# Small pads in SBUF that put the tiles of the three-product matmuls at multiples of 128 bytes

## The chip, the cores and the metric
One NeuronCore of one Trainium2 chip runs the whole program. The metric is the device time of one execution in microseconds. A difference under 0.5% is not told from none here.

## What is computed
A decoder trunk of two layers on 256 tokens of width 1024, in fp32. Cut to what matters:

```
for i in range(2):
    proj = x @ w_in[i]                      # q, k, v, u_ssm, u_pool, three gates
    h = sum(sigmoid(gate_b) * (branch_b @ w_br_b) for b in (attn, ssm, pool)) @ w_o[i]
    x = layer_norm(alpha * x + h)
    x = layer_norm(alpha * x + cross_attention(x, mem))   # 4 heads, 256 memory tokens
    f = swiglu(x)          if i == 0        # width 2816
    f = moe_swiglu(x)      if i == 1        # 8 experts of width 3584, the best 2 of each token
    x = layer_norm(alpha * x + f)
```

The 8 experts hold most of the weights: 336 of the 462 transfers of 1 MB.

## The kernel before
All weights are fp32 and come from HBM in tiles `raw` of 128 partitions x 2048 columns (1 MB), issued on SyncE's queue in the order of use. Up to the second layer's mixer `raw` is one of three buffers of the pool `fifo`; in that layer's cross-attention and in the experts eleven buffers `fx` and the tile `k1` come in turn with them (`wnew`, lines 244 to 257).

A product of fp32 accuracy is made of three fp32r products. Each half of `raw` (128 x 1024) is split once it is needed: ScalarE writes `whi`, the value rounded to fp32r (`hi_of`, line 218), and VectorE writes `wlo = raw - whi` (`lo_of`, line 221). Both have three buffers in the pool `wsp`. The activations are split in the same way (`xhi`/`xlo`, `m_hi`/`m_lo`, `u_hi`/`u_lo`, `hh`/`hl`, `xg0`/`xg1` and so on). TensorE then accumulates three products in PSUM:

```
def mm3(ps, whi, wlo, xhi, xlo, first, last):            # lines 281 to 283
    T.matmul(ps, whi, xhi, start=first, stop=False)
    T.matmul(ps, whi, xlo, start=False, stop=False)
    return T.matmul(ps, wlo, xhi, start=False, stop=last)
```

`T.matmul(out, a, b)` loads `a` (128 columns) as the stationary operand and moves the columns of `b` past it; the trace names them `out<-b,a`. Two arrangements occur. In `mm3` (projections, gates, branches, the gate and up parts of the dense SwiGLU) the weights are stationary and 256 columns of activations move. In `xs_step` (lines 428 to 432) and `mm3_x` (lines 450 to 452) the activations are stationary and 512 (once 256) columns of weights move; `gate_up` of the experts (lines 1301 to 1303) does the same and its `down` calls `mm3_x`. `prepare` gathers an expert's tokens by 128 matmuls with a matrix of ones and zeros (line 1273, 256 columns) and `scatter` puts them back by 64 of 512 columns (lines 1338 and 1339). A few plain fp32 matmuls (attention scores in line 1067, weighted values in line 1100, transposes, the state space) are not split.

Line 238 is the helper `Line`, which keeps a sequence in order; many operations have it as their line. Around the three-product matmuls, attention and the state space are woven into the gates' and branches' projections (`weave`, line 956). The order of each engine's instructions is set when the program is built and is the same for every run.

SBUF is handed out by pools. A pool's tiles lie behind each other along a partition, each rounded up to 32 bytes, and the next pool begins where the last one ends; pools with `side="right"` (`wa`, `kv`, `gg`) grow downwards from the upper end. So a few small tiles in one pool (`halfpi` and `mhalf` in `cp`, the statistics of `sm`, the parameters in `sc`, the routing values of `moe`) set where all pools behind it begin. Slices of the tiles that the fp32r matmuls read begin at multiples of 512 bytes from the tile's start, so a tile's start modulo 128 is that of all its operands.

Of the kernel before, what the change touches and what calls it, by code (L numbers as in the profile page):

```python
# [12 lines left out]
F32 = mybir.dt.float32  # L13
# [7 lines left out]
P = 128  # L21
# [9 lines left out]
NT = 16  # L31
# [5 lines left out]
DFE = 3584  # L37
NEB = DFE // 512
NCE = 42
ALPHA = (2.0 * L) ** 0.25  # L40
EPS = 1e-5
NFIFO = 3
# [14 lines left out]
NPK = PC["bre"][0]  # L57
# [139 lines left out]
def tile_trunk(ctx, tc, x_in, xt_in, memt_in, w_in, par_in, ln_in, lnt_in, wr_in, br_in, cst_in, out):  # L197
    nc = tc.nc

    V, A, T, GP = nc.vector, nc.scalar, nc.tensor, nc.gpsimd  # L200

    cp = ctx.enter_context(tc.tile_pool(name="cp", bufs=1))
    fifo = ctx.enter_context(tc.tile_pool(name="fifo", bufs=NFIFO))
    wsp = ctx.enter_context(tc.tile_pool(name="wsp", bufs=3))
    xp = ctx.enter_context(tc.tile_pool(name="xp", bufs=1))
    sm = ctx.enter_context(tc.tile_pool(name="sm", bufs=2))

    cst = cp.tile([P, NCC], F32, name="cst")

# [100 lines left out]
    def layer_norm_in(l, i, f, end, kind, lp, r):  # L310
# [18 lines left out]
        for m in range(2):  # L329
# [3 lines left out]
            for n in range(2):  # L333
                dv(V.scalar_tensor_tensor, y[:, H[n]], x[:, m, H[n]], ALPHA, f(m, n), op0=ALU.mult, op1=ALU.add)
                if m == 1 and n == 0:
# [57 lines left out]
    GP.memset(mhalf, -0.5)  # L393
    halfpi = cp.tile([P, 1], F32, name="halfpi")
    V.memset(halfpi, math.pi / 2)


    def ws_gemm(nob, kt, act, sink, first=0, w=None):
# [107 lines left out]
    def ssm_params(sp, l, mp, par, par2, tmps, b8, b4, b2):  # L506

        def Q(name):
            if PC[name][0] < NPK:
                return par[:, PC[name][0]:PC[name][1]]  # L510
            return par2[:, PC[name][0] - NPK:PC[name][1] - NPK]

        sh = [P, NT]
        sp["bgh"] = mp.tile([P, 24], F32, name="bgh")
        V.tensor_scalar(sp["bgh"], Q("bg"), 0.5, None, op0=ALU.mult)
        yield
        ntmp = [0]
# [153 lines left out]
    def mixer(l, xt, sc, sp, par, xk):  # L671
        with ExitStack() as es:
# [29 lines left out]
            if sp is None:  # L702
                sp = {}
                pre = ssm_params(sp, l, sc, par, par2, tmps, lambda *a: x.rearrange(
                    "p m (t k h j) -> p m t k h j", t=8, k=4, h=2), b4, wk2)
                next(pre)
# [408 lines left out]
    def ffn(l, xt, sc, mt, kt_):  # L1115
        with ExitStack() as es:
# [8 lines left out]
            tmps = mp.tile([P, 64, NT], F32, tag="sp1", name="tmps", bufs=4)  # L1125
            sp = {}
            steps = ssm_params(sp, l + 1, sc, par, par2, tmps, *[lambda sh, *a, i=i: mp.tile(sh, F32, tag=f"sp{i}", name=a[-1], bufs=(1, 4, 4)[i])
                                         for i in range(3)])

# [40 lines left out]
    def moe(l, xn_hi, xn_lo, pl, dv):  # L1170
        with ExitStack() as es:
            mp = es.enter_context(tc.tile_pool(name="moe", bufs=1, reuse_waits="tile"))
# [2 lines left out]
            psd = es.enter_context(tc.tile_pool(name="mpd", bufs=2, space=PSUM))  # L1175
            pst = es.enter_context(tc.tile_pool(name="mpt", bufs=2, space=PSUM))

            cr = cp.tile([P, NCT - NCA], F32, tag="ca", name="cr")
            nc.sync.dma_start(cr, cst_in[:, NCA:])

# [46 lines left out]
            def weigh():  # L1227
# [21 lines left out]
                V.tensor_copy(cnti, cnt)  # L1249
                GP.tensor_scalar(x, x, ALPHA, None, op0=ALU.mult)  # L1250

# [40 lines left out]
            def gate_up(xg, src):  # L1292
                pg = psg.tile([P, 512], F32, tag="gu", name="pg")
                pu = psg.tile([P, 512], F32, tag="gu", name="pu")
                for gu, ps in enumerate((pg, pu)):
                    for c in range(2):
                        w = wnext(src(2 * gu + c))
                        for kk in range(4):
                            k = 4 * c + kk
                            wh, wl = w(kk * 512, (kk + 1) * 512)  # L1300
                            T.matmul(ps, xg[0][:, k, :], wh, start=(k == 0), stop=False)  # L1301
                            T.matmul(ps, xg[0][:, k, :], wl, start=False, stop=False)  # L1302
                            T.matmul(ps, xg[1][:, k, :], wh, start=False, stop=(k == KD - 1))  # L1303
                sl = wk.tile([P, 512], F32, tag="msl", name="msl", bufs=1)
                A.activation(sl, pg, AF.Silu)
                V.tensor_mul(sl, sl, pu)
                ps = pst.tile([P, 512], F32, tag="tr", name="ps")
                for j in range(4):
                    T.transpose(ps[:, j * P:(j + 1) * P], sl[:, j * P:(j + 1) * P], ident)
                ht_hi = wk.tile([P, 4, P], F32R, tag="hth", name="hth", bufs=2)  # L1310
                ht_lo = wk.tile([P, 4, P], F32R, tag="htl", name="htl", bufs=2)
                p3 = ps.rearrange("p (j t) -> p j t", j=4)
                hi_of(ht_hi, p3)
                lo_of(ht_lo, p3, ht_hi)
                return ht_hi, ht_lo
# [28 lines left out]
            def gsrc(e, nb):  # L1344
                return lambda c: w_in[base + NCE * e + 4 * nb + c]

            def dsrc(e, nb):
                return lambda c: w_in[base + NCE * e + 4 * NEB + 2 * nb + c]

# [46 lines left out]
            with tc.If(n_max > P):  # L1396
                with tc.For_i(0, E, 1) as i:
# [15 lines left out]
                    for nb in range(NEB):  # L1413
                        def src(off):
                            return lambda c: w_in[ds(base + off + c + i * NCE, 1)].rearrange("o p c -> (o p) c")
                        ht = gate_up(xg, src(4 * nb))
# [8 lines left out]
    for l in range(L):  # L1425
# [21 lines left out]
        kvg.__exit__(None, None, None)  # L1447
    dense.close()
    moe(L - 1, *xt)


# [19 lines left out]
```

## Time and profile before

| | |
|---|---|
| runs of the kernel | 1933.56 us median of 3 (1933.01 to 1942.75) |
| the profiled execution | 1936.35 us; its span, first to last instruction, 1934.6 us |
| mean granted TensorE clock | 0.987 |
| busy: PE, PEld, DVE | 1877.8 us (97%), 1630.0 us (84%), 1532.4 us (79%) |
| busy: ACT, POOL | 1282.4 us (66%), 110.9 us (6%) |
| DMA | 503.37 MB, mean 260 GB/s |
| matmuls | 10672 records, each with a weight load |

PE is TensorE's matmuls, PEld its weight loads, DVE VectorE, ACT ScalarE, POOL GpSimd, SP SyncE. A matmul's duration holds its latency, and matmuls overlap, so the time that one costs in a row of them is not its duration but its pitch, the distance of one start to the next. The views used are the stretches (busy time of each engine in a window), the chain of waits (followed back from the last instruction), the list in order of time, and the waits (which engine idled until what).

### The profile page before, as it was taken

The numbers are of one execution on the slowest core, as the hardware profiler recorded it, in microseconds if no ns is written. First come the engines' busy times: TensorE is split into PE (matmuls) and PEld (weight loads), VectorE is DVE, ScalarE is ACT, GpSimd is POOL, SyncE is SP. The second block draws the span as 40 slices with busy tenths as digits, with TensorE's granted clock in tenths as the row PEclk, the third lists the DMA queues.
The fourth block names the chain that finished last, engine by engine and source line by source line (L and its number), as shares of the span: only waits on it lengthen the run. The fifth ranks groups of instructions, "written<-read, shape, count | busy, mean of one in ns | idle before, by whom it ended". The sixth has DMA issues, their size and how long they took to land.

```text
span 1934.6 us, 27897 instructions
## 1 busy us (share of the span) xinstructions
PE 1877.8 (97%) x10672; PEld 1630.0 (84%) x10672; DVE 1532.4 (79%) x1976; ACT 1282.4 (66%) x1673; POOL 110.9 (6%) x111
## 2 busy tenths in 40 slices
PE   7999999999999999998899999999999999999996
PEld 7998998899989988897688888888888888888875
DVE  7774774795557755765899999999999999999987
ACT  5666554556445555554687777777878778787774
POOL 4030000100004300001100000000000000000000
PEclk9999999999999999999999999999999999999998
DMA  7324554444555343594599998999989999899970
GB/s 256 132 90 147 189 211 149 181 175 153 186 185 183 115 161 113 196 408 158 211 375 369 358 376 319 373 375 353 375 321 374 375 356 374 319 375 364 387 271 24
DMA packets 74924, 503.37 MB, mean 260 GB/s; under 512 B 9504, under 2 KB 11808, under 8 KB 15264
## 3 DMA queue, kind: packets, MB, share of 16 engines
q1 hardware_dynamic: 74496, 500.43, 69.0%
q8 instruction: 85, 1.39, 0.3%
q0 software_dynamic: 144, 1.05, 0.2%
q14 instruction: 55, 0.45, 0.1%
q10 hardware_dynamic: 144, 0.05, 0.0%
HBM read 498.34 MB, written 1.05 MB: 258 GB/s over the span
## 4 chain that ended last, share of the span: by engine, by line
PE 89%; DVE 6%; ACT 3%; issue 2%; DMA 0%; POOL 0%; SPq 0%; ACTq 0%; POOLq 0%; DVEq 0%
PE ps L281 8%; PE ps L283 8%; PE ps L282 8%; PE pu L1302 5%; PE dn L450 5%; PE pu L1303 5%; PE pg L1303 5%; PE pu L1301 5%; PE pg L1302 5%; PE dn L451 5%; PE dn L452 5%; PE pg L1301 5%; DVE wlo L221 3%; PE acc L428 2%; PE acc L430 2%; PE acc L432 2%
## 5 line engine op out<-in xcount | busy, mean ns | idle before, releaser
L221 DVE TENSOR_TENSOR wlo<-raw,whi 128x1024 fp32r<-128x1024 f32 x926 | 1118.1, 1229 | 299.0 <-ACT whi L218 284.6
L218 ACT ACTIVATE whi<-raw 128x1024 fp32r<-128x1024 f32 x926 | 974.2, 1060 | 510.0 <-PE ps L282 183.9
L281 PE MATMUL ps<-xhi,whi 128*128 128x256 f32 x992 | 284.9, 289 | 9.0 <-ACT whi L218 8.6
L283 PE MATMUL ps<-xhi,wlo 128*128 128x256 f32 x992 | 284.4, 288 | 3.3 <-DVE wlo L221 3.3
L282 PE MATMUL ps<-xlo,whi 128*128 128x256 f32 x992 | 284.2, 287 | 0.0
L281 PEld LDWEIGHTS ps<-xhi,whi 128*128 128x128 f32 x992 | 192.5, 195 | 10.6 <-ACT whi L218 8.8
L283 PEld LDWEIGHTS ps<-xhi,wlo 128*128 128x128 f32 x992 | 192.7, 195 | 4.6 <-DVE wlo L221 3.8
L282 PEld LDWEIGHTS ps<-xlo,whi 128*128 128x128 f32 x992 | 193.0, 195 | 0.8 <-issue 0.3
L1302 PE MATMUL pu<-wlo,xg 128*128 128x512 f32 x448 | 175.8, 392 | 2.7 <-DVE wlo L221 2.7
L451 PE MATMUL dn<-wlo,hth 128*128 128x512 f32 x448 | 177.9, 400 | 0.1
L1302 PE MATMUL pg<-wlo,xg 128*128 128x512 f32 x448 | 176.3, 394 | 1.4 <-DVE wlo L221 1.4
L1303 PE MATMUL pg<-whi,xg 128*128 128x512 f32 x448 | 175.6, 392 | 0.6 <-DVE xg L1254 0.6
L1301 PE MATMUL pg<-whi,xg 128*128 128x512 f32 x448 | 175.0, 391 | 0.0
L1301 PE MATMUL pu<-whi,xg 128*128 128x512 f32 x448 | 174.7, 390 | 0.0
L1303 PE MATMUL pu<-whi,xg 128*128 128x512 f32 x448 | 174.6, 390 | 0.0
L452 PE MATMUL dn<-whi,htl 128*128 128x512 f32 x448 | 173.8, 391 | 0.0
L450 PE MATMUL dn<-whi,hth 128*128 128x512 f32 x448 | 139.3, 390 | 0.0
L1302 PEld LDWEIGHTS pu<-wlo,xg 128*128 128x128 f32 x448 | 84.0, 188 | 27.6 <-DVE wlo L221 6.6
L1302 PEld LDWEIGHTS pg<-wlo,xg 128*128 128x128 f32 x448 | 84.1, 188 | 24.1 <-DVE wlo L221 3.8
L1301 PEld LDWEIGHTS pu<-whi,xg 128*128 128x128 f32 x448 | 84.1, 188 | 17.8
L450 PEld LDWEIGHTS dn<-whi,hth 128*128 128x128 f32 x448 | 83.9, 188 | 17.9
L1301 PEld LDWEIGHTS pg<-whi,xg 128*128 128x128 f32 x448 | 84.2, 188 | 17.3
(520 smaller groups left out, 2874.9 us busy)
## 6 DMA issues: line engine op xcount, KB each, us to landing
raw<-in_w SPq DMA_DIRECT2D x462, 1024.0 KB, 4.9
lng<-in_ln SPq DMA_DIRECT2D x6, 512.0 KB, 6.5
lnb<-in_ln SPq DMA_DIRECT2D x6, 512.0 KB, 7.3
raw<-in_memt SPq DMA_DIRECT2D x2, 1024.0 KB, 5.1
raw<-in_xt SPq DMA_DIRECT2D x4, 256.0 KB, 5.9
raw<-in_w SPq DMA_DIRECT2D x2, 512.0 KB, 6.3
ux<-us SPq DMA_DIRECT2D x32, 32.0 KB, 2.1
yg<-ux SPq DMA_DIRECT2D x32, 32.0 KB, 1.9
```

Source lines behind the costliest of these rows:

```text
L218: return A.activation(dst, src, AF.Copy, scale=scale)
L221: return V.tensor_sub(dst, src, hi.bitcast(F32))
L281: T.matmul(ps, whi, xhi, start=first, stop=False)
L282: T.matmul(ps, whi, xlo, start=False, stop=False)
L283: return T.matmul(ps, wlo, xhi, start=False, stop=last)
L428: T.matmul(accs[m][n], ah, wh, start=first, stop=False)
L450: T.matmul(ps, ah, wh, start=first, stop=False)
L451: T.matmul(ps, ah, wl, start=False, stop=False)
L452: return T.matmul(ps, al, wh, start=False, stop=last)
L1301: T.matmul(ps, xg[0][:, k, :], wh, start=(k == 0), stop=False)
L1302: T.matmul(ps, xg[0][:, k, :], wl, start=False, stop=False)
L1303: T.matmul(ps, xg[1][:, k, :], wh, start=False, stop=(k == KD - 1))
```

## The change
A function `pad` allocates a tile that nobody reads or writes, as large as is missing to the next multiple of 128 bytes. It is called in the pools `cp`, `sm`, `sc` (inside `ssm_params`, where the pool is called `mp`) and `moe`, and in a new pool `top` at the upper end.

```diff
--- before.py
+++ after.py
@@ -37,6 +37,7 @@
 DFE = 3584
 NEB = DFE // 512
 NCE = 42
+LINE = 128
 ALPHA = (2.0 * L) ** 0.25
 EPS = 1e-5
 NFIFO = 3
@@ -199,11 +200,18 @@
 
     V, A, T, GP = nc.vector, nc.scalar, nc.tensor, nc.gpsimd
 
+
+    def pad(pool, used, name="pad"):
+        if -used % LINE:
+            pool.tile([P, -used % LINE // 4], F32, name=name, bufs=1)
+
     cp = ctx.enter_context(tc.tile_pool(name="cp", bufs=1))
+    pad(ctx.enter_context(tc.tile_pool(name="top", bufs=1, side="right")), 32)
     fifo = ctx.enter_context(tc.tile_pool(name="fifo", bufs=NFIFO))
     wsp = ctx.enter_context(tc.tile_pool(name="wsp", bufs=3))
     xp = ctx.enter_context(tc.tile_pool(name="xp", bufs=1))
     sm = ctx.enter_context(tc.tile_pool(name="sm", bufs=2))
+    pad(sm, 33 * 32)
 
     cst = cp.tile([P, NCC], F32, name="cst")
 
@@ -393,6 +401,7 @@
     GP.memset(mhalf, -0.5)
     halfpi = cp.tile([P, 1], F32, name="halfpi")
     V.memset(halfpi, math.pi / 2)
+    pad(cp, 3 * 32)
 
 
     def ws_gemm(nob, kt, act, sink, first=0, w=None):
@@ -512,6 +521,7 @@
 
         sh = [P, NT]
         sp["bgh"] = mp.tile([P, 24], F32, name="bgh")
+        pad(mp, NPK * 4 + 16 + 24 * 4 + 3 * NT * 4)
         V.tensor_scalar(sp["bgh"], Q("bg"), 0.5, None, op0=ALU.mult)
         yield
         ntmp = [0]
@@ -1175,6 +1185,7 @@
             psd = es.enter_context(tc.tile_pool(name="mpd", bufs=2, space=PSUM))
             pst = es.enter_context(tc.tile_pool(name="mpt", bufs=2, space=PSUM))
 
+            pad(mp, 3 * 32)
             cr = cp.tile([P, NCT - NCA], F32, tag="ca", name="cr")
             nc.sync.dma_start(cr, cst_in[:, NCA:])
 
```

In the built program every engine has the same instructions in the same order, with the same waits; what differs is the addresses. The starts of the tiles modulo 128 bytes, and the fp32r matmuls that an execution makes on them:

| tiles (pool) | before | after |
|---|---|---|
| `whi`, `wlo` (`wsp`), `raw` (`fifo`), `x`, `xhi`, `xlo`, `k1` (`xp`) | 96 | 0 |
| `xg0`, `xg1`, `hth`, `htl`, `pe`, `pet` and other large tiles of `moew` | 96 | 0 |
| `h_hi`, `h_lo`, `qt` (`wa`), `m_hi`, `m_lo` (`kv`), `g_hi`, `g_lo` (`gg`) | 96 | 0 |
| `u_hi`, `u_lo`, `y_hi`, `y_lo`, `o_hi`, `o_lo` of the mixers (`wb`) | 64 | 0 |
| `hh`, `hl` (`ff`), `bt`, `wx`, `lx` (`sc`) | 64 | 0 |
| `o_hi`, `o_lo` of cross-attention in layer 0, `xqt`, `xvv`, `xwt` (`xw`) | 0 | 0 |
| `raw` (`fx`), the constants `cst`, `cstr` (`cp`) | 0 | 0 |

| moving, stationary operand at | columns | matmuls | where |
|---|---|---|---|
| 96, 96 | 256 | 3,776 | `xhi`, `m_hi`, `h_hi` with `whi`, `wlo`; 128 of them gather |
| 64, 96 | 256 | 576 | `u_hi`, `o_hi`, `y_hi` of the mixers |
| 96, 96 | 512 | 4,096 | experts: 2,688 in `gate_up`, 1,344 in `down`, 64 in `scatter` |
| 96, 96 | 512 | 576 | `g_hi`, `xhi`, `m_hi` in `xs_step` and `mm3_x` |
| 96, 64 | 512 | 264 | `hh` in the feed-forward |
| 96, 0 | 512 | 96 | `o_hi` of cross-attention in layer 0 |

After the change all of these are 0, 0. In layer 1 cross-attention keeps its outputs in `m_hi` and `m_lo` instead of tiles in `xw` (line 1094), which is why the same lines 428 to 432 have stationary operands at 0 in layer 0 and at 96 in layer 1.

## Rows read from the trace of the kernel before
**Rows 1.** Stretches: us, busy time of each engine (and instructions), granted clock, DMA share, GB/s.
```profile
0.00:934.30 934.30, 897.41 (x6228) 829.47 (x6229) 616.91 (x1076) 509.78 (x838) 106.70 (x109) 0.98 0.49 176
934.30:1920.50 986.20, 980.41 (x4446) 800.54 (x4444) 906.91 (x885) 772.65 (x835) 2.22 (x1) 1.00 0.90 342
```

**Rows 2.** Chain of waits by line, before and after 934 us.
```profile
by line: PE ps L281 17.0%; PE ps L283 16.7%; PE ps L282 16.6%; PE acc L428 4.6%; PE acc L430 4.6%; PE acc L432 4.5%; PE ps L238 2.3%; issue 1.9%; ACT whi L218 1.8%; DVE wlo L221 1.7%; PE pg L238 1.5%; PE ps L1100 1.5%; PE ps L1067 1.4%; PE 
by line: PE pu L1302 10.1%; PE dn L450 9.9%; PE pu L1303 9.8%; PE pg L1303 9.8%; PE pu L1301 9.7%; PE pg L1302 9.7%; PE dn L451 9.6%; PE dn L452 9.6%; PE pg L1301 9.5%; DVE wlo L221 3.3%; PE ps L1309 2.5%; ACT whi L218 1.5%; DVE x L1340 1.3
```

**Rows 3.** Chain in order of time: start us, us, what; `mm3` on tiles at 96.
```profile
81.73 0.21 PE ps L283
...
86.00 0.21 PE ps L282
...
88.83 0.12 PE ps L281
...
90.15 0.12 PE ps L283
```

**Rows 4.** Stretches: the granted clock around these pieces.
```profile
84.00:86.40 2.40, 2.40 (x14) 2.40 (x12) 0.51 (x1) 0.09 (x1) 0.00 (x0) 0.50 0.00 0
88.80:91.00 2.20, 2.20 (x21) 2.20 (x20) 2.01 (x3) 0.72 (x2) 1.53 (x1) 1.00 0.50 130
```

**Rows 5.** TensorE in order of time, experts: start us, us, engine, line, operation, tiles, shapes.
```profile
1103.63 0.39 PE L1301 MATMUL pg<-whi,xg 128*128 128x512 f32 x1
...
1107.03 0.39 PE L1301 MATMUL pg<-whi,xg 128*128 128x512 f32 x1
```

**Rows 6.** Chain in order of time: three runs of plain fp32 matmuls.
```profile
93.74 3.50 PE pg L238 x32
...
300.22 3.02 PE ps L1067 x14
...
330.81 6.91 PE ps L1100 x32
```

**Rows 7.** TensorE in order of time: a branch's projection, layer 0.
```profile
100.51 0.28 PE L283 MATMUL ps<-u_hi,wlo 128*128 128x256 f32 x1
...
102.52 0.28 PE L282 MATMUL ps<-u_lo,whi 128*128 128x256 f32 x1
```

**Rows 8.** TensorE in order of time: lines 428 to 432, layer 0, layer 1, feed-forward.
```profile
348.76 1.09 PE L428 MATMUL acc<-whi,o_hi 128*128 128x512 f32 x4
...
350.62 0.63 PE L430 MATMUL acc<-wlo,o_hi 128*128 128x512 f32 x2
...
895.78 1.07 PE L428 MATMUL acc<-whi,m_hi 128*128 128x512 f32 x4
...
897.59 0.62 PE L430 MATMUL acc<-wlo,m_hi 128*128 128x512 f32 x2
...
402.11 1.10 PE L428 MATMUL acc<-whi,hh 128*128 128x512 f32 x4
...
403.98 0.63 PE L430 MATMUL acc<-wlo,hh 128*128 128x512 f32 x2
```

**Rows 9.** Waits in the experts: who waited for whom, us, times, longest.
```profile
ACT whi L218 <- PE pu L1303: 69.7, 128, 1.1
DVE wlo L221 <- ACT whi L218: 59.3, 190, 1.5
```

**Rows 10.** VectorE's subtractions by tile: count, duration ns min/median/max, first and last start.
```profile
L221 DVE TENSOR_TENSOR o_lo<-ps,o_hi x4: 691/692/692, 333.6 to 338.4; 128x512 fp32r<-128x512 f32 x4
...
L221 DVE TENSOR_TENSOR m_lo<-ps,m_hi x4: 692/692/694, 883.7 to 888.4; 128x512 fp32r<-128x512 f32 x4
...
L221 DVE TENSOR_TENSOR wlo<-raw,whi x926: 1193/1225/3377, 8.4 to 1913.9; 128x1024 fp32r<-128x1024 f32 x186
```

**Rows 11.** Stretches: a full DMA queue, and the experts.
```profile
840.00:850.00 10.00, 10.00 (x85) 9.97 (x84) 4.25 (x4) 4.92 (x8) 0.00 (x0) 1.00 1.01 425
1000.00:1200.00 200.00, 199.32 (x912) 163.55 (x911) 185.39 (x183) 157.57 (x172) 0.00 (x0) 1.00 0.94 356
```

## The prediction, made before the changed kernel ran
> **What bounds the kernel now.** I read the stretches first. Up to 934.3 us (projections, attention, state space, cross-attention, dense SwiGLU) TensorE is busy for 897 of 934 us, VectorE for 617; from 934.3 to 1920.5 us (the experts) TensorE for 980 of 986 us, VectorE for 907, at the full granted clock [rows 1]. Busy time of a pipelined TensorE proves little, so the chain of waits comes next: before 934 us half of it is the three lines of `mm3` (17.0 + 16.7 + 16.6%) and 13.7% the three of `xs_step`; after it nine lines of matmuls hold 9.5 to 10.1% each, and only 3.3% is VectorE's `wlo` [rows 2]. So the pitch of the three-product matmuls, start to start, sets the time, and it is read from the rows by dividing a distance of starts by the matmuls between.
>
> 256 columns, both operands 96 bytes past a multiple of 128: from 88.83 to 90.15 us eleven steps, 120 ns each [rows 3]. 256 columns take 106.7 ns at 2.4 GHz, so 13 ns are something else. It is no constant of the instruction: at the granted clock of 0.50 the same matmuls on the same tiles go from 81.73 to 86.00 us in twenty steps of 213.5 ns, which is 256 columns at 1.2 GHz and nothing more [rows 3, 4]. 512 columns, both operands at 96: fifteen steps in 3.40 us, 226.7 ns against 213.3 [rows 5]. The excess is 13.3 ns in both, 32 columns at 2.4 GHz, whatever the length. 32 fp32 columns are 128 bytes. A run that starts at 96 touches one 128-byte piece more (9 instead of 8, 17 instead of 16), and 9 and 17 pieces of 13.3 ns are 120 and 226.7 ns. My reading, a conclusion from these numbers: the moving operand arrives in whole 128-byte pieces at a fixed rate, which TensorE at 2.4 GHz just uses up.
>
> Three more rows bear on it. The plain fp32 matmuls of line 1100 (operands at 0) stand as 32 records in 6.91 us, 216 ns each, and those of line 1067, whose moving operand lies at 96, as 14 in 3.02 us, 216 again [rows 6]: they take two columns' time per column, and an extra piece hides. With the moving operand at 64 and the stationary one at 96, 17 steps take 2.01 us, 118 ns [rows 7]: the phase matters, but 64 gives only 2 ns. And with the moving operand at 96, the stationary one's phase counts too: 8 steps of line 428 to 432 take 1.86 us with it at 0 (layer 0), 1.81 with it at 96 (layer 1), 1.87 in the feed-forward with it at 64, so 232.5, 226 and 234 ns [rows 8].
>
> **The change, part by part.** No instruction is added, dropped or moved; only addresses change. Afterwards both operands of each of the 9,192 three-product matmuls, of the 128 that gather an expert's tokens and of the 64 that scatter them, lie at 0 (the change's table has the counts). No fp32r matmul on a pair (0, 0) can be read in this trace at full clock, so I bound the new pitch. *512 columns:* not below 213.3 (columns at 2.4 GHz), not above 234 (the dearest pair); I take 216, what 512 columns' time costs in the plain fp32 records, where no piece is short [rows 6]. *256 columns:* not below 106.7; above, 127 (120 and the 7 ns that a stationary operand at 0 or 64 cost). Here the weight load of each matmul comes near: 32 records whose 32 columns hide behind their loads take 3.50 us, 109 ns each [rows 6]. I take 110.
>
> Before the experts:
> - 256 columns, pair (96, 96): 3,776 x (120 - 110) = 37.8 us, the 128 gathers in it.
> - 256 columns, pair (64, 96): 576 x (118 - 110) = 4.6 us.
> - 512 columns, pair (96, 96): 576 x (227 - 216) = 6.3 us.
> - 512 columns, stationary at 0 or 64: 360 x (234 - 216) = 6.5 us.
>
> Together 55.2 us, on the chain only where TensorE is not fed late. The chain shows 1.8% for `whi`, 1.7% for `wlo` and 1.9% for issue [rows 2], and the woven side work (attention, state space) keeps its own lengths; where it ends last the gain becomes a wait. I count 85%: **47 us**.
>
> The experts and the scatter: 4,096 x (227 - 216) = 45.1 us on the chain. Late next is `wlo`: for each half tile ScalarE writes `whi`, then VectorE `wlo`, into three buffers each. VectorE is busy 907 of 986 us; it idles 79, of which 59 are waits for `whi`, and ScalarE waits for a free buffer, 70 us behind one product of `gate_up` alone [rows 1, 9], so both now follow TensorE. VectorE gets no faster: the same subtraction takes 692 ns with its SBUF tiles at 0 and at 96 [rows 10]. With all 45 us gained VectorE would be 907 of 941 us busy, 96%; TensorE will meet late `wlo` tiles at block ends. I leave a third there: **30 us**, VectorE then at 907/956, 95%.
>
> DMA is no bound: it moves 356 GB/s in the experts and moved 425 with a full queue [rows 11]; 356 x 986/956 is 367. ScalarE (773 of 986 us), POOL and SP only follow [rows 1]. The pads cost at most 96 bytes a partition and no instruction.
>
> Sum: 47 + 30 = 77 us. The profiled execution took 1936.35 us (span 1934.6), so it would take 1859; it lies 2.8 us above the median of the runs, 1933.56, and from that the forecast is 1933.56 - 77 = **1857 us**.
>
> The Trainium skill ("TensorE: Matmul & The Clock Gate", Back-to-back issue gap) gives a warm gap of N/2.4 + 2.5 ns, so 109 and 216 by estimate; with 109 the first line would be 41.5 us instead of 37.8. The plain fp32 rows agree with it, and the 120 and 227 ns of the fp32r rows do not.
>
> **The rivals.**
> *VectorE takes over the experts.* Against it: 79 us of idle time there. For it: from 1000 to 1200 us it is busy 185.4 of 200 us, 93%, at a steady pace [rows 11]. If it can't pass 93%, the stretch ends at 907/0.93 = 975 us, 11 gained: 47 + 11 = 58, **1876 us**.
> *No piece of 128 bytes.* What counts is that both operands start alike, and (0, 0) is no better than (96, 96). For it: 96 is itself a multiple of 32, and the pairs that start alike are cheaper than the mixed ones of 512 columns. Against it: 118 ns for (64, 96), and that the excess is exactly 128 bytes' worth. Then 360 x 7 ns are gained and 576 x 2 lost: **1932 us**.
> The Trainium skill ("SBUF — State Buffer", Specifications) speaks for this rival: its SBUF lines are 16 bytes long, and 96 is the start of one, so a contiguous run would gain nothing. The 13.3 ns of excess speak against it.
> *Half a gain.* Phase 0 gives what 64 shows, 2 ns: (3,776 + 4,672) x 2 ns and 360 x 9 ns, 20 us: **1914 us**.
> *Slower: the stationary operand at 0 is dear in itself.* Place: every weight load. Price: 7 ns, the difference of 0 and 64 against 96 in [rows 8], on 4,672 matmuls of 512 columns that have it at 96 now: 33 us; on the shorter ones between nothing and as much. It decides if the moving operand's phase gives less than those 7 ns. Against it: a weight load of 128 columns has 216 ns to hide in. **1966 us**.
> That the change doesn't do what it says can be excluded: the addresses in the built program are at 0.
>
> **How the numbers follow.** Forecast 0.63, VectorE 0.17, half a gain 0.06, no piece 0.09, slower 0.05. The range covers the first two, 0.80: below, 55.2 and 45.1 passed almost whole, 98 us, 1835; above, VectorE's case with 60% of the first sum, 33 + 11 = 44 us, 1890. A change of under 0.5% (10 us) can't be told from none. Faster: 0.63 + 0.17 + 0.06 = 0.86; same 0.09; slower 0.05.
>
> **What would show it.** Right: eleven steps of `mm3` in 1.2 us instead of 1.32, fifteen in the experts in 3.24 instead of 3.40, layer 0 and layer 1 alike in lines 428 to 432, unchanged rows at clock 0.50, `wlo` at 1225 ns [rows 10] with less idle time before it and more waits of TensorE for it, first stretch near 887 us, experts near 956. Wrong: pitches still at 120 and 227 (no piece), 233 in the experts (slower), or pitches as forecast with a stretch of the experts over 970 us (VectorE).

## The result and the profile after

The changed kernel is **slower**: 1956.77 us median of 7 runs (1950.98 to 1957.6) against 1938.29 (1933.01 to 1942.88) of the kernel before beside it, a ratio of 1.0089 [1.0068, 1.0111]; ratios and their intervals here come from all runs of both kernels, and a ratio need not be the quotient of the two medians beside it. The forecast was 1857 us, range 1835 to 1890. The profiled execution took 1957.5 us, with a span of 1955.7 against 1934.6, at the same mean granted clock, 0.987.

The same two stretches of the kernel after (us, busy time of PE, PEld, VectorE, ScalarE and POOL, granted clock, DMA share, GB/s), cut again where the experts begin and where the last scatter ends:

```profile
0.00:938.30 938.30, 900.67 (x6228) 830.61 (x6229) 618.50 (x1077) 509.94 (x839) 108.05 (x109) 0.98 0.49 176
938.30:1941.50 1003.20, 998.46 (x4446) 805.34 (x4444) 910.70 (x883) 772.10 (x835) 1.46 (x1) 1.00 0.89 336
```

Against [rows 1] the experts take 17.0 us more (1003.2 against 986.2), the rest 4.0 more, and TensorE's busy time grows by about as much (18.1 and 3.3). VectorE's grows by 4 and 2 us, ScalarE's hardly. The chain of waits in the experts, by line:

```profile
by line: PE pu L1313 9.8%; PE pg L1314 9.8%; PE pg L1313 9.7%; PE pu L1314 9.7%; PE pu L1312 9.6%; PE pg L1312 9.5%; PE dn L459 9.2%; PE dn L460 9.1%; PE dn L461 9.1%; DVE wlo L229 4.6%; PE ps L1320 2.2%; ACT whi L226 2.0%; issue 1.3%; DVE 
```

It is the chain of [rows 2] with the lines moved by 11 (or by 8 and 9): the nine matmul lines hold nearly everything, `wlo` 4.6 instead of 3.3%. No new wait took over. The matmuls themselves got longer, as TensorE in order of time shows in the experts and in lines 437 to 441 of layer 1 (the lines 428 to 432 of before):

```profile
1110.67 0.40 PE L1312 MATMUL pg<-whi,xg 128*128 128x512 f32 x1
...
1114.16 0.39 PE L1312 MATMUL pg<-whi,xg 128*128 128x512 f32 x1
```

```profile
899.25 1.09 PE L437 MATMUL acc<-whi,m_hi 128*128 128x512 f32 x4
...
901.11 0.62 PE L439 MATMUL acc<-wlo,m_hi 128*128 128x512 f32 x2
```

Fifteen steps of 512 columns lie between the first two rows: 3.49 us, 232.7 ns each, where [rows 5] had 226.7. Eight lie between the second two: 1.86 us, 232.5 ns, where [rows 8] had 1.81 us. Over all expert matmuls the mean from start to start is 232.6 ns against 227.9: 4,096 x 4.7 = 19.3 us, of which 17.0 show in the stretch. And 256 columns of x, on the chain in order of time:

```profile
90.62 0.12 PE ps L289
...
91.94 0.12 PE ps L291
```

Eleven steps in 1.32 us, 120 ns, the same as in [rows 3]. The excess that the change was to remove is there as before. VectorE's `wlo` also stayed at 1225 ns, the median by tile [rows 10].

The times fall into place with another variable than the starts modulo 128. From the tiles' addresses in the two built programs I took for each kind of matmul the **distance**: address of the moving operand minus address of the stationary one, modulo 256. Before, x, the experts, memory and gates had distance 0 (512 columns 227 ns, 256 columns 120), the feed-forward's `hh` 32 and layer 0's `o_hi` 224 (232.5 to 234), `u_hi` 224 (118). After, every operand starts at a multiple of 128, but the weights at a multiple of 256 and the expert and right-hand pools at an odd multiple of 128: distance 128, 232 ns. Only x kept distance 0, and 120 and 227 ns (the latter in the 96 products of 512 columns in which x is stationary). That is theory **D**; the rival **P** is the prediction's own terms, a starting phase of one operand that is dear or cheap by itself.

### The profile page after: what moved, and what is told of

It is laid out like the page before. It is cut to its first block, busy times and chain, and to the rows that moved or that the text cites. A ratio compares the mean times of both kernels' runs of the same rounds, so it can differ in the third digit from the quotient of the medians.

```text
span 1955.7 us, 27897 instructions
## 1 busy us (share of the span) xinstructions
PE 1899.1 (97%) x10672; PEld 1636.0 (84%) x10672; DVE 1537.8 (79%) x1976; ACT 1282.0 (66%) x1673; POOL 111.5 (6%) x111
## 4 chain that ended last, share of the span: by engine, by line
PE 88%; DVE 7%; ACT 3%; issue 2%; DMA 0%; POOL 0%; DVEq 0%; ACTq 0%; POOLq 0%
PE ps L289 8%; PE ps L291 8%; PE ps L290 8%; PE pu L1313 5%; PE pg L1314 5%; PE pg L1313 5%; PE pu L1314 5%; PE pu L1312 5%; PE pg L1312 5%; PE dn L459 5%; PE dn L460 5%; PE dn L461 5%; DVE wlo L229 3%; PE acc L441 2%; PE acc L437 2%; PE acc L439 2%
## 5 line engine op out<-in xcount | busy, mean ns | idle before, releaser
L1314 PE MATMUL pg<-whi,xg 128*128 128x512 f32 x448 | 177.7, 397 | 0.6 <-DVE xg L1265 0.6
L1312 PE MATMUL pu<-whi,xg 128*128 128x512 f32 x448 | 176.9, 395 | 0.0
L1312 PE MATMUL pg<-whi,xg 128*128 128x512 f32 x448 | 176.9, 395 | 0.0
L1314 PE MATMUL pu<-whi,xg 128*128 128x512 f32 x448 | 176.8, 395 | 0.0
```

## The experiments

**TensorE alone, all distances.** Resident tiles, one block of 48 equal matmuls after the other, here in outline (not the code itself):

```python
block(st[0], mv[d], 128 stationary columns, 512 moving)   # d: 0, 32, ... 224 modulo 256; st[0] at 128
block(st[0], mv[d], 128, 256)
block(st[s], mv[0], 128, 512)                             # s: 128, 160, 192, 224
block(st[0] as fp32, mv[d] as fp32, 128, 256)
```

> Not the network: TensorE alone, blocks of 48 equal matmuls on resident tiles, nothing else at work; the stationary tile begins at 128 modulo 256 bytes, the moving one at each multiple of 32. In the two traces a 512-column three-product matmul took 227 ns where moving and stationary operand begin at the same address modulo 256, 233 to 234 at a distance of plus or minus 32, 232 at 128. Theory D (the distance between the two operands sets the pitch): the same values at these three distances, so blocks of 512 columns differ by 5 to 8 ns with the distance, the lowest at 0; and shifting the stationary tile instead gives the same table. Theory P (the starting phase of an operand by itself, as my prediction had it): moving operands at 32, 64 and 96 modulo 128 at 216 ns or at 227, those at multiples of 128 at the other, whatever the distance. Theory C (the excess over 213.3 ns comes from the three engines that read and write beside TensorE in the kernel): every block at about 214 ns, no difference by address.

TensorE in order of time; each row is a block (start us, us, tiles, shapes), and the start of the next row less its own, over 48, is the pitch (the fp32 rows hold 96):

```profile
65.53 11.35 PE L39 MATMUL ps<-mvd,sta 128*128 128x512 f32 x48
76.72 11.05 PE L39 MATMUL ps<-mve,sta 128*128 128x512 f32 x48
87.61 11.37 PE L39 MATMUL ps<-mvf,sta 128*128 128x512 f32 x48
98.81 11.16 PE L39 MATMUL ps<-mvg,sta 128*128 128x512 f32 x48
109.81 11.37 PE L39 MATMUL ps<-mvh,sta 128*128 128x512 f32 x48
121.02 5.86 PE L39 MATMUL ps<-mva,sta 128*128 128x256 f32 x48
126.72 5.80 PE L39 MATMUL ps<-mvb,sta 128*128 128x256 f32 x48
...
143.69 5.92 PE L39 MATMUL ps<-mve,sta 128*128 128x256 f32 x48
149.44 5.82 PE L39 MATMUL ps<-mvf,sta 128*128 128x256 f32 x48
...
160.76 5.91 PE L39 MATMUL ps<-mvh,sta 128*128 128x256 f32 x48
166.50 11.18 PE L39 MATMUL ps<-mva,sta 128*64 128x512 f32 x48
...
277.41 11.16 PE L39 MATMUL ps<-mva,stc 128*128 128x512 f32 x48
288.41 11.36 PE L39 MATMUL ps<-mva,std 128*128 128x512 f32 x48
299.61 65.82 PE L39 MATMUL ps<-mva,sta 128*128 128x512 f32 x288
...
427.43 20.88 PE L39 MATMUL ps<-mve,sta 128*128 128x256 f32 x96
448.15 20.88 PE L39 MATMUL ps<-mvf,sta 128*128 128x256 f32 x96
```

At 512 columns, from 65.53 us: distance 224: 233.1 ns, **0: 226.9**, 32: 233.3, 64: 229.2, 96: 233.5. Moving the stationary tile instead gives the same table: 64 (277.41): 229.2, 32 (288.41): 233.3. At 256 columns distance 128 (121.02) gives 118.8, 0 (143.69) 119.8 and 96 (160.76) 119.6: 0 is now among the dearest. Plain fp32 takes 215.8 ns (20.72 us over 96) everywhere. So theory D holds with TensorE alone. C falls, since 226.9 and 119.8 need no other engine. P falls: a moving operand at 0 modulo 128 takes 226.9 ns (`mve` on `sta`), 229.2 (`mva` on `stc`) or 233.3 (`mva` on `std`) by the distance alone, and no start gives 216. Two kinds of block are not among these rows. With the moving start 4 to 24 bytes further on (distances 132 to 152) 512 columns take 233 to 236 ns. With 64 stationary columns instead of 128 they take 228 to 232 ns and 230 at distance 0, so the low at 0 was seen with full-width weights only.

**One pad alone, behind the constants.** x, weights and experts go together from 224 to 0 modulo 256:

```diff
+    pad(cp, 3 * 32)
```

> Only the 32-byte pad behind the constants: weights (wsp), x tiles and both expert pools move together by 32 bytes, to multiples of 256, so in the experts and the row products the two operands keep distance 0; the right-hand pools stay, so 576 memory, read-out and attention matmuls get distance 32. Theory D: 512-column expert matmuls stay at 227 ns, an expert stays at 120 to 124 us, the total within about 5 us of before (1935 to 1944 against 1938). Theory P in the form of my rival (stationary or moving operand dear at a multiple of 128 bytes): experts at 232 ns per matmul, 122 to 126 us each, the total 1953 to 1960 as with the whole change.

Measured 1936.78 against 1936.25 us, ratio 1.0005 [0.9992, 1.0017]. The expert stretch:

```profile
933.10:1920.50 987.40, 981.79 (x4445) 801.65 (x4444) 906.75 (x883) 772.42 (x835) 1.42 (x1) 1.00 0.89 342
```

987.4 us, as before [rows 1], and in order of time the experts' matmuls (line 1308 is before's 1301) keep their pitch:

```profile
1102.63 0.39 PE L1310 MATMUL pg<-whi,xg 128*128 128x512 f32 x1
...
1105.12 0.40 PE L1309 MATMUL pg<-wlo,xg 128*128 128x512 f32 x1
```

Eleven steps take 2.49 us, 226 ns. Both operands of x's and the experts' products start at a multiple of 256 here, and neither a gain nor a loss comes of it; P in either sign falls again. The right-hand pools stayed where they were: the 480 products of 512 columns on memory and gates went from distance 0 to 32 and, by the mean from start to start, from 227 to 233 ns, some 3 us, too little to show in the total.

**The expert pools alone, by 128 bytes.** No start modulo 128 differs from the kernel before:

```diff
+            mp.tile([P, 32], F32, name="pad")
```

> The kernel before with one 128-byte pad at the start of the expert pools alone: no start modulo 128 changes anywhere, only the distance between expert activations and weights goes from 0 to 128 modulo 256. Theory D: 4,096 expert matmuls at 232 instead of 227 ns, each expert 2 to 2.5 us longer, the total 16 to 20 us over before (about 1955 against 1938), all of the change's loss. Theory P: nothing changes, total within 2 us of before.

Measured 1952.86 against 1936.25 us, 1.0094 [1.0066, 1.0122]: 16.6 us between the medians, nearly the change's whole loss. The expert stretch is that of the change:

```profile
931.40:1935.00 1003.60, 998.89 (x4446) 806.28 (x4444) 910.80 (x883) 772.19 (x835) 1.46 (x1) 1.00 0.89 336
```

**192 bytes there instead of 128** (distance 64):

```diff
+            mp.tile([P, 48], F32, name="pad")
```

> As the run with the expert pads alone, but with 192 bytes in place of 128: the moving weights lie 64 modulo 256 above the stationary activations in all 4,096 expert matmuls, no start modulo 128 is a multiple of 128. Theory D with the table measured on TensorE alone (228.9 ns at 64, 226.7 at 0, 232 to 233 at 128): 2 ns more per expert matmul than before, total 6 to 10 us over before, about half of what 128 cost. A theory in which any distance but 0 costs alike: 16 to 20 us over. A theory by the 128-byte phase alone (activations at 32 modulo 128, weights at 96): no telling, but then not half of the loss by chance.

Measured 1942.48 against 1936.02 us, 1.0023 [1.0012, 1.0035]; the stretch is 6.1 us longer than before:

```profile
939.60:1931.90 992.30, 986.82 (x4446) 803.51 (x4444) 908.33 (x883) 771.82 (x835) 1.45 (x1) 1.00 0.89 340
```

The table's order holds in the kernel: 0, then 64, then 128. Over all expert matmuls the mean from start to start is 229.3 ns, which over 4,096 is 5.7 us more than before. The ratio's interval is 2.3 to 6.8 us, mostly below the 6 to 10 that I expected.

**What the 13.3 ns are.** TensorE alone, distance 0, one thing varied from block to block (columns, stationary columns, banks, accumulation, rows, bf16).

> Not the network: TensorE alone again, all operands at distance 0 modulo 256, blocks of 48. One thing varies from block to block: moving columns 64 to 512; stationary columns 16 to 128 at 512 and at 256 moving columns; the result in one or in two alternating banks; every matmul by itself instead of accumulating; two pairs of operands in turn; 64 rows instead of 128; bf16. Theory F (a fixed price per three-product matmul, not a piece of the address): 13.3 ns over columns / 2.4 GHz at every column count, 66.7 ns at 128 columns and 173.3 at 384, and unchanged by banks, accumulation and pairs. Theory W (the excess is the weight load's reads among the stream's): it falls with the stationary columns, to under 216 ns for 512 moving columns at 16 of them. Theory B (the excess is the accumulation in one bank): gone with two banks or with single matmuls.

VectorE adds each block's result at its end, so its rows in order of time mark the block ends; the difference over 48 is the pitch. The shape in a row is the result's, stationary by moving columns:

```profile
61.08 0.42 DVE L44 TENSOR_TENSOR acc<-acc,ps 128x256 f32<-128x256 f32 x1 [5.41 <-PE ps L41]
68.12 0.49 DVE L44 TENSOR_TENSOR acc<-acc,ps 128x320 f32<-128x320 f32 x1 [6.62 <-PE ps L41]
76.44 0.56 DVE L44 TENSOR_TENSOR acc<-acc,ps 128x384 f32<-128x384 f32 x1 [7.84 <-PE ps L41]
86.36 0.62 DVE L44 TENSOR_TENSOR acc<-acc,ps 128x448 f32<-128x448 f32 x1 [9.36 <-PE ps L41]
97.28 0.69 DVE L44 TENSOR_TENSOR acc<-acc,ps 128x512 f32<-128x512 f32 x1 [10.31 <-PE ps L41]
108.39 0.68 DVE L44 TENSOR_TENSOR acc<-acc,ps 16x512 f32<-16x512 f32 x1 [10.41 <-PE ps L41]
...
152.66 0.41 DVE L44 TENSOR_TENSOR acc<-acc,ps 32x256 f32<-32x256 f32 x1 [5.04 <-PE ps L41]
158.10 0.41 DVE L44 TENSOR_TENSOR acc<-acc,ps 64x256 f32<-64x256 f32 x1 [5.03 <-PE ps L41]
...
227.54 0.29 DVE L65 TENSOR_TENSOR acc<-acc,ps 128x128 f32<-128x128 f32 x1 [2.36 <-PE ps L64]
232.78 0.42 DVE L65 TENSOR_TENSOR acc<-acc,ps 128x256 f32<-128x256 f32 x1 [4.95 <-PE ps L64]
243.14 0.69 DVE L65 TENSOR_TENSOR acc<-acc,ps 128x512 f32<-128x512 f32 x1 [9.94 <-PE ps L64]
```

320 columns: 146.7 ns, 384: 173.3, 512: 227.5, each 13.3 to 14.2 over columns / 2.4 GHz, as 256 columns with 120; but 448: 206.7, 20 over. With 64 stationary columns 256 moving ones take 113.3, 6.6 over, but with 16 it is 116.7 again; with 16 stationary columns 512 moving ones take 231.5, more than with 128. bf16 has 109.2 and 215.8, only 2.5 over. Two banks, single matmuls, two pairs of operands in turn and 64 rows changed nothing (about 227 and 120 ns from start to start once a block runs evenly). So F holds from 256 columns on but for 448; the blocks of 64 to 192 columns can't speak for it, since the granted clock fell in them (last section). B falls, and W holds in part at 256 columns and fails at 512. The excess is there in fp32r matmuls, not in bf16 ones, and the runs above showed no start of an operand that removes it. That it has to do with the weight load is only argued, from the 256-column blocks; its cause stays open.

**Own weights or the next ones.** Blocks that alternate between two pairs of operands:

```python
block([(S0, M0), (S1 + d, M1 + d)])   # own distance 0, to the next weights -d and d in turn
block([(S0, M0 + d), (S1 + d, M1)])   # own distance d and -d in turn, to the next weights 0
block([(S0, M0 + d)])                 # also d = 256 bytes to 2048
```

> Not the network: TensorE alone, blocks of 48 matmuls that alternate between two pairs of operands. Which weights does a moving operand stand against: its own, or those of the next matmul, which are loaded while it streams? In the run with the expert pads alone the scatter matmuls (both operands in the expert pool, own distance 0, neighbours at 128) took 232 ns, as if the own distance were not what counts. Theory N (next): blocks whose own distance is 0 and whose distance to the next weights is 128 take 232 to 233 ns at 512 columns, and blocks with own distance 128 and 0 to the next take 227; at 256 columns 118 to 119 and 120. Theory O (own): the other way round, 227 and 232. Theory M (both, or a state that lasts over many matmuls): both near 230 or 232. Blocks at distances 256, 512, 768, 1024 and 2048 bytes tell whether 256 is the modulus: then all 227 and 120.

VectorE's rows again, the ends of the blocks:

```profile
22.83 0.69 DVE L38 TENSOR_TENSOR acc<-acc,ps 128x512 f32<-128x512 f32 x1 [21.44 <-PE ps L37]
33.71 0.69 DVE L38 TENSOR_TENSOR acc<-acc,ps 128x512 f32<-128x512 f32 x1 [10.19 <-PE ps L37]
44.83 0.69 DVE L38 TENSOR_TENSOR acc<-acc,ps 128x512 f32<-128x512 f32 x1 [10.43 <-PE ps L37]
56.02 0.69 DVE L38 TENSOR_TENSOR acc<-acc,ps 128x512 f32<-128x512 f32 x1 [10.51 <-PE ps L37]
...
150.81 0.42 DVE L38 TENSOR_TENSOR acc<-acc,ps 128x256 f32<-128x256 f32 x1 [5.23 <-PE ps L37]
162.16 0.69 DVE L38 TENSOR_TENSOR acc<-acc,ps 128x512 f32<-128x512 f32 x1 [10.93 <-PE ps L37]
173.20 0.69 DVE L38 TENSOR_TENSOR acc<-acc,ps 128x512 f32<-128x512 f32 x1 [10.35 <-PE ps L37]
...
217.69 0.69 DVE L38 TENSOR_TENSOR acc<-acc,ps 128x512 f32<-128x512 f32 x1 [10.46 <-PE ps L37]
228.84 0.69 DVE L38 TENSOR_TENSOR acc<-acc,ps 128x512 f32<-128x512 f32 x1 [10.47 <-PE ps L37]
...
402.67 0.42 DVE L38 TENSOR_TENSOR acc<-acc,ps 128x256 f32<-128x256 f32 x1 [5.07 <-PE ps L37]
413.57 0.69 DVE L38 TENSOR_TENSOR acc<-acc,ps 128x512 f32<-128x512 f32 x1 [10.49 <-PE ps L37]
```

All at 0: 226.7 ns (22.83 to 33.71). Own 0, next 128: 236.5 (to 162.16). Own 128, next 0: 230.0 (to 173.20). Both 128: 232.3 (to 228.84). So theory M: neither distance alone decides, and with 128 both must be 0 for 227 ns. It is no simple sum. With 64 bytes and 192 in turn, own 0 takes 231.7 (to 44.83) and next 0 takes 233.1 (to 56.02), the other way round than with 128; and a block whose distances, own and next alike, are 0 and 192 in turn takes 227.5 (from 290.83 to 301.75, not among these rows), as if all were 0. Distances of 256 to 2048 bytes count as 0 (512 bytes, to 413.57: 227.1), so 256 is the modulus.

**A version built from the table.** x is allocated ahead of the weights and kept 64 bytes apart from them, which puts the 256-column products at distance 192:

```diff
-    wsp = ctx.enter_context(tc.tile_pool(name="wsp", bufs=3))
     xp = ctx.enter_context(tc.tile_pool(name="xp", bufs=1))
+    pd = ctx.enter_context(tc.tile_pool(name="pd", bufs=1))
+    pd.tile([P, 16], F32, name="pad")
+    wsp = ctx.enter_context(tc.tile_pool(name="wsp", bufs=3))
```

> A version built from the table: the x pool is allocated ahead of the weights with a 64-byte pad between, so the 256-column moving activations (xhi, xlo, h, m) lie at distance 192 to the stationary weights (117.8 ns against 119.9 at 0 on TensorE alone) and the 512-column moving weights at 64 to the right-hand pools (228.9 against 226.7); the experts stay at 0. 2,976 + 96 + 576 matmuls less 2.1 ns each is 7.7 us, 576 + 96 + 96 more 2 ns each is 1.5 us. Theory D with TensorE on the path in the dense stages: 5 to 6 us under before, 1930 to 1932 against 1936. If VectorE's conversions set the dense stages instead, or the table does not carry over: within 2 us of before.

**1924.14 against 1936.02 us, 0.9939 [0.9923, 0.9955]**, more than expected. The stretches, and two pieces of x's products in order of time:

```profile
0.00:919.40 919.40, 880.97 (x6228) 810.97 (x6229) 616.59 (x1076) 510.44 (x838) 108.78 (x109) 0.98 0.49 179
919.40:1906.00 986.60, 980.79 (x4446) 800.46 (x4444) 907.36 (x885) 772.83 (x835) 2.48 (x1) 1.00 0.89 342
```

```profile
420.00 0.28 PE L284 MATMUL ps<-xlo,whi 128*128 128x256 f32 x1
...
423.41 0.28 PE L283 MATMUL ps<-xhi,whi 128*128 128x256 f32 x1
...
599.77 0.28 PE L283 MATMUL ps<-xhi,whi 128*128 128x256 f32 x1
...
603.05 0.28 PE L285 MATMUL ps<-xhi,wlo 128*128 128x256 f32 x1
```

The stretch before the experts fell from 934.3 to 919.4 us, 14.9 less; the experts stayed. 29 steps take 3.41 us in the first piece, 117.6 ns, the table's value; in the second 3.28 us, 113.1 ns, with the same distances. Half of x's products run in that second way (median 114, mean 115.6), which TensorE alone never showed at this distance. 2,976 x (119.9 - 115.6) + 576 x (119.8 - 114.9) is 15.6 us, less 576 x 1.6 for the 512-column ones, 14.7. That 14.9 meets this so closely is in part luck, for the clock helped: before its experts this execution spent 31 us at the granted clock of 0.50, that of the kernel before 38. At 213.5 ns a step instead of 120 [rows 3, 4] the 7 us are worth 3 (an estimate), so some 12 of the 14.7 arrived, as between the two medians (11.9).

**The same with 32 bytes more ahead of the feed-forward and 224 ahead of cross-attention**, so that their 360 products stand at 0:

```diff
+            mp.tile([P, 8], F32, name="pad", bufs=1)
+            wk.tile([P, 56], F32, name="pad", bufs=1)
```

> The last version with two pads more, 32 bytes at the start of the feed-forward pool and 224 at the start of the cross-attention pool, so that the 264 + 96 matmuls of 512 columns that stood at distance 32 or 224 (233 ns) stand at 0 (227 ns). Theory D: 360 times 6 ns, 2.2 us under the last version, about 1928 to 1930. If these stages wait for other engines: no difference to the last version.

1922.39 us, 0.9925 [0.9912, 0.9939]. Their pitch fell from 233 to 227 ns; the 1.7 us between the medians fit 2.2, but the two intervals overlap, so the gain in time is not shown.

**And with 224 bytes ahead of the state-space pool:**

```diff
+            wb.tile([P, 56], F32, name="pad")
```

> The last full version with one pad more, 224 bytes at the start of the pool of the state-space stage and the attention outputs, so that 576 matmuls of 256 columns (u, o, y) go from distance 224 (118.5 ns) to 192 (115 to 116 ns measured in that version for x). Theory D with TensorE on the path: 576 times 3 ns, 1.7 us under it, about 1920.5 against 1922.4, ratio to before 0.991 to 0.993. If those stages wait for VectorE or ScalarE: no difference.

1920.6 against 1934.73 us, 0.9931 [0.9918, 0.9944]: the pitch of u, o and y fell to 114 to 116 ns, and the total can't be told from the version before it. Each of these three beats both kernels of the case.

## Why the prediction was wrong

- **"The pitch of the three-product matmuls, start to start, sets the time": right.** 19.3 us of longer matmuls made the experts 17.0 us longer, and of 14.7 us of shorter ones in the dense stages some 12 arrived.
- **"A run that starts at 96 touches one 128-byte piece more": this step failed**, and with it the new pitches of 110 and 216 ns, on which all terms hung. 13.3 ns is the time of 32 columns, but it is also there with both operands at a multiple of 256 (226 to 227 and 120 ns with one pad alone), and no start in the blocks alone took less than 226 ns for 512 columns. That one number fitted exactly was no test; 448 columns with 20 ns would have been one. Another was at hand: a run that starts at 64 touches 9 pieces too, so the 118 ns of [rows 7] already spoke against the count.
- **The terms of the sum.** 3,776 x 10 ns: x stayed at 120, so nothing of it. 576 x 8 (118 to 110): 118 became 119. 576 x 11 (227 to 216): 480 became 232, a loss of 2.4 us, and x's 96 stayed at 227. 360 x 18: 233 became 232. 4,096 x 11: became 4.7 ns the other way, 19.3 us. The bound of 213.3 to 234 for the 512-column pitch held, at its other end. The shares that were to arrive (85% before the experts, two thirds in them) had no gain to act on.
- **[Rows 7, 8], read by the starts modulo 128,** were read by the wrong variable. 118 ns at (64, 96) and 232 to 234 ns with the stationary tile at 0 or 64 are the distances 224 and 32, for which the blocks alone give 118.3 ns (256 columns) and 233 ns (512).
- **The rival "no piece"** was nearest. "What counts is that both operands start alike" is right for 512 columns, and its outcome, no change, is what the first pad alone gave (1.0005). But alike modulo 128 is not alike modulo 256, and there the change separates what stood together.
- **The rival "slower"** had the sign and nearly the size (1966 us) with the wrong cause: the stationary operand at 0 costs nothing when the moving one is there too, and the loss came whole with no operand at a new start modulo 128.
- **VectorE's third of the experts' gain** was never put to the test, since no version made the experts' matmuls shorter; when they grew, 2 of 19 us were hidden. `wlo` at 1225 ns was right.
- The Trainium skill ("TensorE: Matmul & The Clock Gate", Back-to-back issue gap) gives N/2.4 + 2.5 ns. The bf16 blocks agree (109.2, 215.8); no fp32r block of 512 columns reached its 216 at any distance. 216 was also what I had taken as the new pitch, from the plain fp32 rows.

The 4.0 us before the experts are pitch and clock together. 480 x 5 ns is 2.4 of them. For the rest: the kernel before and the two versions that move the expert pools alone have identical dense stages, and began their experts at 934.3, 931.4 and 939.6 us after 38, 30 and 47 us at the granted clock of 0.50. Less 0.44 of that time, what a step loses at that clock (213.5 ns instead of 120), all three begin between 918 and 919 us, and the changed kernel (938.3, with 41 us) at 920. That is an estimate; the kernel with one pad alone comes out at 923, 2 to 3 us later than its pitches explain.

## What to carry to other kernels

Ask of two operands that are read together how far apart they lie, not only how each is aligned: pads that align every tile can separate a pair that stood well, and a pad in one pool against another moves thousands of instructions by 5 ns each. If a number fits a mechanism exactly, look for a second row that the mechanism forbids before summing over it. A 500-us kernel of equal blocks, one address varied, would have settled this before a byte was padded.

## What was not expected of the hardware

The pitch of an fp32r matmul depends on moving less stationary address modulo 256: at 512 columns 226.7 ns at 0, 229 at 64, 232 to 234 otherwise; at 256 columns 120 at 0 and at 96, 117 to 119 otherwise. This holds for 128 stationary columns; plain fp32 shows nothing of it. In the kernel, one distance (192) runs in two ways, at 113 or 118 ns a step, and changes between them; what picks one, and what the 256 bytes are in the chip, stays open. And in the blocks alone the granted clock fell from 2.4 GHz to 0.50, the 1.2 GHz level, at 35.3 us, while the block of 64 moving columns ran, and rose again at 52.4 us, in the block of 192. TensorE and its weight loads were busy without a gap before the fall and after it:

```profile
31.00:35.30 4.30, 4.30 (x41) 4.30 (x40) 0.69 (x1) 0.00 (x0) 0.00 (x0) 1.00 0.00 0
35.40:46.90 11.50, 11.50 (x56) 11.50 (x55) 0.22 (x1) 0.00 (x0) 0.00 (x0) 0.50 0.00 0
```

The 48 matmuls of 128 columns, from 36.99 to 47.27 us, took 214 ns each, four times their columns at 2.4 GHz.
